# MLP output kernel: four factor sets in the result's places, two pools for the second half's factors, a later x

## The chip, the core and the metric

One core of a Trainium2 chip runs the whole layer. The time is the device time of one execution in microseconds (us), the median of the runs shown. A profile is one further execution, taken by the hardware profiler; its span runs from its first to its last instruction. PE is TensorE (matmuls), ACT is ScalarE, DVE is VectorE, POOL is GpSimd, and SP only issues transfers. The 16 DMA engines carry what the queues of SP and POOL issue.

## The reference

One decoder layer for 2048 positions of width 1024, all in float32:

```python
def squared_relu_mlp(h, w1, w2):
    a = jax.nn.relu(h @ w1)
    return (a * a) @ w2
...
        h = rms_norm(x, mix_norm_pre[l])
        m = hybrid_mixer(h, w_in[l], conv_w[l], conv_b[l], w_rgate[l], b_rgate[l],
                         w_igate[l], b_igate[l], lru_lambda[l], w_out[l])
        x = x + rms_norm(m, mix_norm_post[l])
        h = rms_norm(x, mlp_norm_pre[l])
        x = x + rms_norm(squared_relu_mlp(h, w_ff_in[l], w_ff_out[l]), mlp_norm_post[l])
```

The mixer joins dilated attention (8 heads) with a gated linear recurrence; its result goes through `w_out`, the out-projection. The MLP is 1024 to 4096 to 1024.

## The kernel before

**Halves.** After the mixer's input work, the layer goes through two halves of 1024 positions, hf = 0 and 1. `half(hf)` does the out-projection (`OutProj`, eight tiles t of 128 positions: the products L820 to L822, then two norms and the residual in `finish`) and the MLP's first product (`mlp_in`). `mlp_out` does the second product with `w2`. The second half's attention runs between, woven into the first half's `mlp_out`. So the order in time is: half 0, `mlp_out` 0 with the attention of half 1, out-projection of half 1, `mlp_in` 1, `mlp_out` 1.

**Matmuls.** Each float32 operand is split into a high part (a cast on ACT) and a low part (a subtraction on DVE or POOL, in place where the load landed), and a product is three matmuls: high by high, high by low, low by high. The 2 x 2 block products of the MLP are seven (m = 1 to 7) in the manner of Strassen. `mlp_in` works on pairs (0 to 15); of each it stores sums for the left factors, in DRAM: squares `sq` (L1061) and their sums `as` (L1062), both stored by POOL; the sums of `w2` (loaded L1071 as `w2s`) go to DRAM likewise.

**Sets.** `mlp_out` runs over 7 m x 16 j, a set each: a factor `a` and a factor `b`, 256 KB each, loaded by SP (L1128) into the place of the low part, then cast (L1218 in half 0, L54 in half 1) and subtracted (L1220, L55). Twelve matmuls use a set (L1135 to L1137). `load` picks the set's place by the number `at`: in half 0 one of four in turn, in half 1 one of sixteen by j. `sh.pair` and `sh.s` are places that also serve the factors of `mlp_in`, and `e` tiles are the half's own. A load can start once the last reader of its place is done:

```python
        at = j if hf else (m_at[m] * NJ + j) % 4
            if at < GB // 2:
                hi, lo = sh.pair(f"{x}{n}", (P, TB))
```

Loads run three sets ahead of the products, in both halves (`range(3)`, `made[i + 3]`). `take` moves a finished block from PSUM into the result rows `y`, whose eight tiles (128 x 1024) are allocated when half 0's product begins. `finish` squares them for the norm (L84), takes the root (L1171), scales (L1177), and lets POOL add the residual by a load (L1178) and store the result (L1179).

**What sets the order.** PE's order is as written. On ACT, DVE and SP the order is as written within `interleave` (the attention woven into `mlp_out` 0: eight sets first, FIRSTFILL = 32 products, then the units of the attention with their loads of masks, L365 and L367, of queries `qs`, L429, of keys `kh`, `kl`, L440, of values `vb`, L445, `va`, L461 and, on POOL, L466). Elsewhere a scheduler decides, by the readiness it reckons for each instruction; `issue_after` bars an instruction from an earlier position than another's. Each engine and each queue works in its order and waits where the next cannot start.

**Around the out-projection of half 1.** The output weights (`woL`, L756) are loaded among the last sets of `mlp_out` 0. `mix_columns` loads the mixer's result for a tile t (`m`, L794), ACT casts it (L54), POOL subtracts (L55). `OutProj` loads `x` (L828) and the gains (L811) and leaves their order to the scheduler.

Of the kernel before, what the change touches and what calls it, by code (L numbers as in the profile page):

```python
# [800 lines left out]
class OutProj:  # L801


    def __init__(self, tc, sh, p, scr, hf, wo, order, x, g2, g3):
        self.nc, self.sh, self.p, self.scr, self.hf, self.wo, self.order, self.x = tc.nc, sh, p, scr, hf, wo, order, x
        self.ahead = self.load(0)
        self.gb = []
        for n, src in (("2", g2), ("3", g3)):
            self.gb.append([sh.s(f"g{n}b{hf}_{i}", (P, TB)) for i in range(2)])
            for i, t in enumerate(self.gb[-1]):  # L810
                self.nc.sync.dma_start(out=t, in_=src[:, i * TB:(i + 1) * TB].partition_broadcast(P))  # L811
# [13 lines left out]
    def load(self, t):  # L825
        tt = self.hf * NQH + t
        xt = self.sh.w(f"xt{tt}")
        self.nc.sync.dma_start(out=xt, in_=self.x[tt * P:(tt + 1) * P, :])  # L828
        return xt
# [264 lines left out]

def mlp_out(tc, sh, p, cst, scr, hf, w2, g4, out):

# [12 lines left out]
    def factors(m, j):  # L1109
        parts = load(m, j)  # L1110
        for hi, lo in parts:
            split_there(nc, hi, lo)
        return [*parts[0], *parts[1]]

    def load(m, j):
        n = f"{hf}_{m}_{j}"
        at = j if hf else (m_at[m] * NJ + j) % 4
        parts = []
        for x, src in (("a", scr["a"][hf][j][:, SCR[m]]),
                       ("b", scr["w2"][j][:, plain[m]] if m in plain else scr["b"][j][:, SCR_B[m]])):  # L1120
            if at < GB // 2:
                hi, lo = sh.pair(f"{x}{n}", (P, TB))
            elif at < (GB + SB // 2) // 2:
                hi, lo = [sh.s(f"{x}{n}{y}", (P, TB), F32R) for y in "HL"]
            else:
                hi, lo = [p.tile([P, TB], F32R, tag="e", bufs=4 * NJ - 2 * GB - SB, name=f"{x}{n}{y}") for y in "HL"]
            with tc.issue_after(cst["load"].ins) if "load" in cst else contextlib.nullcontext():
                cst["load"] = nc.sync.dma_start(out=f32(lo), in_=src)  # L1128
            parts.append((hi, lo))
        return parts  # L1130
# [76 lines left out]
    if hf == 0:  # L1207
# [13 lines left out]

        for i in range(3):
            made[i] = load(*sets[i])
        for q in range(4 + LEAD):
            part(q)
        yield
        y += [p.tile([P, D], F32, tag=f"y{t}", name=f"y{hf}_{t}") for t in range(NQH)]
        for i, (m, j) in enumerate(sets):
            if j == 0:
                if m in (1, 2, 7):  # L1230
                    o = [sh.bank(x, f"o{hf}_{m}_{t}") for t, x in enumerate("AOAA")]
                if m == 2:
                    gains()
            if i + 3 < len(sets):
                made[i + 3] = load(*sets[i + 3])
            (ah, al), (bh, bl) = made[i]
            for t in range(n4):
                product(o[t], t, j, (ah, al, bh, bl), m in (1, 2, 7))
                part(4 * i + t + 4 + LEAD)
                if j == NJ - 1:  # L1240
                    take(m, t, o[t])
                    if m in (2, 4):
                        jobs.append(finish(t if m == 2 else n4 + t))
# [6 lines left out]
        return  # L1250
    ahead = [factors(order[0], j) for j in range(3)]
    yield
# [90 lines left out]
FIRSTFILL = 32  # L1343
LEAD = 4
NJ = FT // 2
KH = KT // 2
# [4 lines left out]
def trunk(tc, x, xT, g1, g2, g3, g4, w_in, conv_w, conv_b, w_r, b_r, w_i, b_i, lam, w_out, w1, w2,  # L1351
# [11 lines left out]
    with (  # L1363
# [112 lines left out]
        def half(hf, wo, mx):  # L1476

            with contextlib.ExitStack() as st:
# [3 lines left out]
                with contextlib.nullcontext():  # L1482

                    place = [po.tile([P, 4, TB], F32, name="place1")] if hf else [
                        po.tile([P, KT, P], F32, name=f"place0_{j}") for j in range(2)]
                    op = OutProj(tc, sh, po, scr, hf, wo, order, x, g2, g3)

# [38 lines left out]
        with per, tc.manual_schedule(engines={mybir.EngineType.PE}):  # L1526
# [13 lines left out]
            end = half(1, wo, ready)  # L1540
            with sb("y1", "left") as p:
                rest = mlp_out(tc, sh, p, cst, scr, 1, w2, g4, out)
                next(rest)
                run_all(end)
                run_all(rest)
# [63 lines left out]
```

## Time and profile before

| | us |
|---|---|
| median of the runs (3: 2290.64 to 2295.60) | 2292.86 |
| the profiled execution | 2294.62 |
| its span | 2292.5 |
| PE busy in the span | 2182.9 (95%) |
| DVE, ACT, POOL busy | 1507.5 (66%), 1233.6 (54%), 461.7 (20%) |

What remains of the profiled execution's time outside its span is 2.1 us. PE is busy for nearly the whole span, so a change shows in the time where PE waits or works at a lower granted clock; the chain of waits has PE on 62% of it and transfers on 11%. Busy time of PE counts a matmul for as long as it was in the array, so at half the clock the same work shows as more busy time.

### The profile page before, as it was taken

To read this page: it belongs to the slowest core of one execution; us is meant where nothing else is said; L and a number is where in the kernel's file an instruction comes from. 1 tells how busy PE (TensorE), PEld (TensorE's weight loads), DVE (VectorE), ACT (ScalarE), POOL (GpSimd) and SP (SyncE) were. 2 spreads that over 40 slices of the span, in tenths; PEclk is the share of its full clock that TensorE was granted. 3 is DMA by queue.
4 is the path that set the end of the run, shared out by engine and by line. 5 is a ranking of instruction groups with operands and counts; after the bars stand their busy time and mean duration, and the time that the engine had idled before them with its cause. 6 is when DMAs were issued, how large, how long until landed. Compare 5 with 4: busy or idle time off the path is not lost.

```text
span 2292.5 us, 30706 instructions
## 1 busy us (share of the span) xinstructions
PE 2182.9 (95%) x10264; PEld 1781.9 (78%) x10264; DVE 1507.5 (66%) x2900; ACT 1233.6 (54%) x2489; POOL 461.7 (20%) x549
## 2 busy tenths in 40 slices
PE   8999999989999899998999999989999999999998
PEld 6678888767788677786788787767878888788887
DVE  6757466897468876774667676766775656545556
ACT  7647465654344654553666666754455555554542
POOL 5543416454023100001001010123200000000003
PEclk9999999999999999998999999999999999999999
DMA  8365674637755667768677777777454444676665
GB/s 290 90 194 177 189 235 154 187 111 229 207 170 175 229 240 280 292 241 270 215 204 222 221 239 198 210 228 232 159 199 138 166 138 156 231 256 193 193 193 183
DMA packets 217550, 466.15 MB, mean 203 GB/s; under 512 B 22464, under 2 KB 77152, under 8 KB 211120
## 3 DMA queue, kind: packets, MB, share of 16 engines
q1 hardware_dynamic: 188624, 329.52, 46.2%
q0 software_dynamic: 28768, 134.66, 16.7%
q8 instruction: 81, 1.33, 0.2%
q14 instruction: 77, 0.63, 0.1%
HBM read 329.75 MB, written 151.13 MB: 210 GB/s over the span
## 4 chain that ended last, share of the span: by engine, by line
PE 62%; DMA 11%; DVE 9%; issue 7%; ACT 5%; POOL 2%; SPq 0%; DVEq 0%; POOLq 0%; ACTq 0%
PE o L1136 7%; PE o L1135 7%; PE o L1137 7%; PE za L996 3%; PE za L997 3%; PE za L998 3%; PE z L198 3%; PE z L199 3%; PE z L200 3%; PE m L822 2%; PE m L821 2%; PE m L820 2%; DMA w2s<-in_dram 2%; PE zc L996 2%; PE zc L997 2%
## 5 line engine op out<-in xcount | busy, mean ns | idle before, releaser
L198 PE MATMUL z<-hH,wH 128*128 128x512 f32 x640 | 261.0, 408 | 13.8 <-ACT wH L54 6.8
L199 PE MATMUL z<-hL,wH 128*128 128x512 f32 x640 | 259.4, 406 | 0.3 <-DVE hL L173 0.3
L200 PE MATMUL z<-hH,wL 128*128 128x512 f32 x640 | 258.4, 405 | 0.0
L198 PEld LDWEIGHTS z<-hH,wH 128*128 128x128 f32 x640 | 122.0, 191 | 49.0 <-ACT wH L54 7.1
L199 PEld LDWEIGHTS z<-hL,wH 128*128 128x128 f32 x640 | 121.9, 190 | 30.3 <-issue 4.1
L200 PEld LDWEIGHTS z<-hH,wL 128*128 128x128 f32 x640 | 121.9, 190 | 29.7 <-issue 4.6
L409 ACT ACTIVATE smB<-smB,stB 128x128 f32<-128x128 f32 (+3 forms) x128 | 71.6, 560 | 79.4 <-DVE stB L403 79.1
L1001 ACT ACTIVATE sq<-sq 128x512 f32<-128x512 f32 x93 | 58.8, 632 | 95.4 <-DVE sq L1005 95.2
L55 POOL TENSOR_TENSOR wL<-wraw,wH 128x512 fp32r<-128x512 f32 x58 | 82.5, 1438 | 77.8 <-ACT wH L54 75.0
L1061 POOL DMA_DIRECT2D sa<-sq x31 | 16.5, 532 | 401.8 <-ACT sq L1002 401.0
L55 DVE TENSOR_TENSOR tlB<-pT_B,thB 128x384 fp32r<-128x384 f32 x96 | 57.1, 599 | 49.6 <-ACT thB L54 45.5
L54 ACT CAST wH<-wraw 128x512 fp32r<-128x512 f32 (+1 forms) x81 | 46.9, 611 | 60.3 <-PE z L199 30.2
L409 ACT ACTIVATE sm<-sm,stA 128x256 f32<-128x256 f32 (+1 forms) x128 | 63.1, 495 | 29.3 <-DVE stA L403 29.0
L1002 ACT ACTIVATE sq<-sq 128x512 f32<-128x512 f32 x124 | 76.7, 629 | 2.4
L1072 DVE TENSOR_TENSOR w2s<-w2s 128x512 f32<-128x512 f32 x64 | 44.1, 689 | 34.2 <-DMA w2s<-in_dram 33.3
L1169 POOL TENSOR_TENSOR y<-y,g4b 128x512 f32<-128x512 f32 x8 | 13.0, 1654 | 262.8 <-ACT junk_y L84 262.8
L403 DVE CUSTOM_DVE_ANT_0 smB<-SB,mask_b 128x128 f32<-128x128 f32 (+3 forms) x128 | 59.4, 483 | 5.8 <-PE pT_B L377 5.4
L996 PE MATMUL za<-hHT,f_6H 128*128 128x512 f32 x128 | 51.7, 404 | 9.0 <-ACT sq L1035 8.9
L55 DVE TENSOR_TENSOR tlA<-pT,thA 128x512 fp32r<-128x512 f32 (+1 forms) x64 | 42.4, 670 | 26.3 <-ACT thA L54 26.0
L607 PE MATMUL oB<-thB,vb 128*128 128x256 f32 x192 | 48.6, 282 | 10.4 <-ACT thB L54 9.7
L54 ACT CAST thB<-pT_B 128x384 fp32r<-128x384 f32 x96 | 48.6, 510 | 18.3 <-PE pT_B L377 10.0
L377 PE MATMUL pT_B<-ident,smB 128*128 128x128 f32 x320 | 52.8, 282 | 2.7 <-DVE tlB L55 0.9
(567 smaller groups left out, 7082.3 us busy)
## 6 DMA issues: line engine op xcount, KB each, us to landing
sa<-as POOLq DMA_DIRECT2D x32, 1024.0 KB, 6.2
w1r<-in_dram SPq DMA_DIRECT2D x58, 512.0 KB, 4.5
sa<-sq POOLq DMA_DIRECT2D x31, 768.0 KB, 3.9
wraw<-in_dram SPq DMA_DIRECT2D x79, 256.0 KB, 3.6
w2s<-in_dram SPq DMA_DIRECT2D x16, 1024.0 KB, 8.1
sb<-w2s POOLq DMA_DIRECT2D x16, 1024.0 KB, 6.4
kh<-sk SPq DMA_DIRECT2D x24, 512.0 KB, 5.1
kl<-sk SPq DMA_DIRECT2D x24, 512.0 KB, 6.5
```

The lines of the kernel that those rows point to most:

```text
L54: return (nc.scalar.copy(out=hi, in_=src), (lo_eng or nc.vector).tensor_tensor(out=lo, in0=src, in1=f32(hi), op=ALU.subtract))
L55: (lo_eng or nc.vector).tensor_tensor(out=lo, in0=src, in1=f32(hi), op=ALU.subtract))
L198: pe.matmul(z, hi[:, k, :], hh, start=(k == 0), stop=False)
L199: pe.matmul(z, hi[:, k, :], hl, start=False, stop=False)
L200: pe.matmul(z, lo[:, k, :], hh, start=False, stop=(k == KT - 1))
L409: s.activation(out=sm[:, c0:c0 + w], in_=sm[:, c0:c0 + w], func=AF.Exp, scale=-1.0, bias=st[:, 0, u, cols[j]:cols[j] + 1], accum_out=st[:, ...
L996: pe.matmul(o, hi[:, k], bh[:, k], start=start and k == 0, stop=False, skip_group_check=True)
L997: pe.matmul(o, hi[:, k], bl[:, k], start=False, stop=False, skip_group_check=True)
L1002: s.activation(out=z, in_=z, func=AF.Square)
L1135: pe.matmul(o, ah[:, ts], bh, start=fresh and j == 0, stop=False, skip_group_check=True)
L1136: pe.matmul(o, ah[:, ts], bl, start=False, stop=False, skip_group_check=True)
L1137: pe.matmul(o, al[:, ts], bh, start=False, stop=j == NJ - 1, skip_group_check=True)
```

## The change

1. **First half.** The first four sets go into tiles with the tags of `y` (y0 to y7, the high part in the left half, the low part in the right). The result's own tiles are allocated when the first block is taken, after these sets have been read. Eight sets are loaded before the product begins, not three, and from the sixth set on the loads again run three ahead. The ring of four places turns by `(i + 3) % 4`.
2. **Second half.** The sets' places turn by `(j + 4) % 16`, the `e` tiles lie in two pools (`y1` and `z1`), and six sets are loaded ahead for the first product, not three.
3. **x of the second out-projection.** Its loads are barred from a position ahead of the last set's load of the first half.

```diff
@@ class OutProj @@
-    def __init__(self, tc, sh, p, scr, hf, wo, order, x, g2, g3):
+    def __init__(self, tc, sh, p, scr, hf, wo, order, x, g2, g3, late=None):
...
+        self.tc, self.late = tc, late
...
-        self.nc.sync.dma_start(out=xt, in_=self.x[tt * P:(tt + 1) * P, :])
+        with self.tc.issue_after(self.late.ins) if self.late else contextlib.nullcontext():
+            self.nc.sync.dma_start(out=xt, in_=self.x[tt * P:(tt + 1) * P, :])
@@ mlp_out, load @@
-        at = j if hf else (m_at[m] * NJ + j) % 4
+        i = m_at[m] * NJ + j
+        at = (j + 4) % NJ if hf else (i + 3) % 4
...
-            if at < GB // 2:
+            if not hf and i < 4:
+                t = p.tile([P, D], F32R, tag=f"y{2 * i + (x == 'b')}", name=f"{x}{n}")
+                hi, lo = t[:, :TB], t[:, TB:]
+            elif at < GB // 2:
...
-                hi, lo = [p.tile([P, TB], F32R, tag="e", bufs=4 * NJ - 2 * GB - SB, name=f"{x}{n}{y}") for y in "HL"]
+                q = pl if at < EARLY7 else p
+                hi, lo = [q.tile([P, TB], F32R, tag="e", bufs=4 * (EARLY7 - 4 if at < EARLY7 else NJ - EARLY7),
+                                 name=f"{x}{n}{y}") for y in "HL"]
@@ mlp_out, half 0 @@
-        for i in range(3):
+        for i in range(8):
             made[i] = load(*sets[i])
...
-        y += [p.tile([P, D], F32, tag=f"y{t}", name=f"y{hf}_{t}") for t in range(NQH)]
...
-            if i + 3 < len(sets):
+            if 5 <= i < len(sets) - 3:
                 made[i + 3] = load(*sets[i + 3])
...
+                    if not y:
+                        y += [p.tile([P, D], F32, tag=f"y{t}", name=f"y{hf}_{t}") for t in range(NQH)]
@@ mlp_out, half 1 @@
-    ahead = [factors(order[0], j) for j in range(3)]
+    ahead = [factors(order[0], j) for j in range(EARLY7 - 4)]
@@ calls @@
+EARLY7 = 10
-                    op = OutProj(tc, sh, po, scr, hf, wo, order, x, g2, g3)
+                    op = OutProj(tc, sh, po, scr, hf, wo, order, x, g2, g3, cst["load"] if hf else None)
-            with sb("y1", "left") as p:
-                rest = mlp_out(tc, sh, p, cst, scr, 1, w2, g4, out)
+            with sb("y1", "left") as pl, sb("z1", "left") as p:
+                rest = mlp_out(tc, sh, p, cst, scr, 1, w2, g4, out, pl)
```

Lines move by up to 11 in the changed file (L1128 is L1137 there, L1171 L1180, L828 L830).

**How it moves instructions.** PE's order stays. The names below are tiles with the product m and the set j (`a_1_6L`: factor a, m = 1, j = 6, low part); the half's number is left out.

SP, start of the first half's output product, before:

```order
L1128 DMA a_1_2L<-sa_2_123 128x512
L1128 DMA b_1_2L<-sw_171 128x512
L365 DMA mask_a_9591<-in_dram 128x256
L367 DMA mask_b_9593<-in_dram 128x512
L1128 DMA a_1_3L<-sa_3_124 128x512
L1128 DMA b_1_3L<-sw_172 128x512
L429 DMA qs_0_9633<-sq_0_75 128x1x1024
L1128 DMA a_1_4L<-sa_4_125 128x512
L1128 DMA b_1_4L<-sw_173 128x512
L440 DMA kh_0_9634<-sk_0_79 128x1x1024
```

The same place in the changed kernel, from the last factor of set 6 on (the other loads of sets 0 to 6 stand above, as one run behind the last load of `w2s`):

```order
L1137 DMA b_1_6L<-sw_175 128x512
L1137 DMA a_1_7L<-sa_7_128 128x512
L1137 DMA b_1_7L<-sw_176 128x512
L365 DMA mask_a_9613<-in_dram 128x256
L367 DMA mask_b_9615<-in_dram 128x512
L429 DMA qs_0_9641<-sq_0_75 128x1x1024
L440 DMA kh_0_9642<-sk_0_79 128x1x1024
L440 DMA kh_0_9642<-sk_0_83 128x1x1024
L440 DMA kl_0_9643<-sk_0_79 128x1x1024
L440 DMA kl_0_9643<-sk_0_83 128x1x1024
L1137 DMA a_1_8L<-sa_8_129 128x512
```

The loads of sets 3 to 7 stand ahead of the masks, and the loads of queries and keys come as one run behind set 7.

POOL there, before (`sb` is a store of `w2`'s sums):

```order
L1073 DMA sb_168<-w2s_9397 128x2048
L1061 DMA sa_14_135<-sq_14_9352 128x1536
L1062 DMA sa_14_135<-as_14_9572 128x2048
L466 DMA va_0_9779<-sv_0_91 32x4x256 x8
L1061 DMA sa_15_136<-sq_15_9404 128x1536
L1062 DMA sa_15_136<-as_15_9579 128x2048
```

and in the changed kernel:

```order
L1075 DMA sb_168<-w2s_9397 128x2048
L1063 DMA sa_14_135<-sq_14_9352 128x1536
L466 DMA va_0_9763<-sv_0_91 32x4x256 x8
L1064 DMA sa_14_135<-as_14_9594 128x2048
L1063 DMA sa_15_136<-sq_15_9404 128x1536
L1064 DMA sa_15_136<-as_15_9601 128x2048
```

The eight loads of `va` stand ahead of pair 14's store of `as`, where they stood behind it.

SP in the last product of the first half (m = 4), before; `swo` holds the output weights:

```order
L1128 DMA b_4_8L<-sb_161 128x512
L756 DMA woL_5_14251<-swo_206 128x1024
L828 DMA xt_14638<-in_dram 128x1024
L828 DMA xt_14700<-in_dram 128x1024
L1128 DMA a_4_9L<-sa_9_130 128x512
L1128 DMA b_4_9L<-sb_162 128x512
```

In the changed kernel, at the end of the same product; `g2b` and `g3b` are gains, `m_0` is the first tile of the second out-projection:

```order
L1137 DMA a_4_15L<-sa_15_136 128x512
L1137 DMA b_4_15L<-sb_168 128x512
L830 DMA xt_14630<-in_dram 128x1024
L830 DMA xt_14692<-in_dram 128x1024
L812 DMA g2b_0_14632<-in_dram 128x512
L812 DMA g2b_1_14633<-in_dram 128x512
L812 DMA g3b_0_14636<-in_dram 128x512
L812 DMA g3b_1_14637<-in_dram 128x512
L794 DMA m_0_0L<-smix_104 128x4x128
```

The two loads of x stand twenty loads of sets and weights later, and the four gains, which stood behind the loads of `m_2`, ahead of `m_0`.

ACT where the second out-projection begins, before; `junk_y` are the squares of the result's rows 4 to 7:

```order
L54 CAST m_0_0H<-m_0_0L 128x512
L54 CAST m_0_4H<-m_0_4L 128x512
L84 ACTIVATE junk_y_14540,ss_14536<-y_4_9599 128x1024
L54 CAST m_1_0H<-m_1_0L 128x512
L54 CAST m_1_4H<-m_1_4L 128x512
L1171 ACT_TABLE_LOAD
L1171 ACTIVATE ss_14537<-ss_14536,eps 128x1
L84 ACTIVATE junk_y_14562,ss_14558<-y_5_9600 128x1024
L1171 ACTIVATE ss_14559<-ss_14558,eps 128x1
L84 ACTIVATE junk_y_14576,ss_14572<-y_6_9601 128x1024
L1171 ACTIVATE ss_14573<-ss_14572,eps 128x1
L84 ACTIVATE junk_y_14590,ss_14586<-y_7_9602 128x1024
```

and in the changed kernel:

```order
L84 ACTIVATE junk_y_14532,ss_14528<-y_4_10133 128x1024
L1180 ACT_TABLE_LOAD
L1180 ACTIVATE ss_14529<-ss_14528,eps 128x1
L84 ACTIVATE junk_y_14554,ss_14550<-y_5_10134 128x1024
L1180 ACTIVATE ss_14551<-ss_14550,eps 128x1
L84 ACTIVATE junk_y_14568,ss_14564<-y_6_10135 128x1024
L1180 ACTIVATE ss_14565<-ss_14564,eps 128x1
L84 ACTIVATE junk_y_14582,ss_14578<-y_7_10136 128x1024
L54 CAST m_0_0H<-m_0_0L 128x512
L54 CAST m_0_4H<-m_0_4L 128x512
L1180 ACTIVATE ss_14579<-ss_14578,eps 128x1
L54 CAST m_1_0H<-m_1_0L 128x512
```

The casts of `m_0` stood ahead of all four squares and stand behind them now; those of `m_1` follow.

## Rows read from the trace of the kernel before

**Rows 1.** The table by stage (windows), core 0: from:to, us, busy time of each engine.
```profile
core 0: us, PE busy (x) PEld busy (x) DVE busy (x) ACT busy (x) POOL busy (x), PEclk, DMA share, GB/s
1020.00:1040.00 20.00, 20.00 (x88) 16.12 (x87) 11.28 (x19) 9.35 (x17) 1.59 (x3) 1.00 0.94 326
1040.00:1057.00 17.00, 17.00 (x77) 14.08 (x76) 10.00 (x16) 8.88 (x17) 0.53 (x1) 1.00 0.44 140
1057.00:1106.20 49.20, 35.74 (x133) 27.08 (x132) 19.53 (x37) 18.10 (x35) 6.58 (x12) 0.83 0.96 315
1520.00:1547.00 27.00, 19.83 (x77) 15.27 (x76) 15.68 (x21) 12.41 (x22) 14.26 (x18) 0.87 1.01 334
1974.40:1992.20 17.80, 13.86 (x52) 10.21 (x51) 7.45 (x12) 6.02 (x10) 1.18 (x3) 0.90 1.01 365
1992.20:2285.00 292.80, 292.80 (x1292) 242.17 (x1291) 168.06 (x279) 139.32 (x254) 19.31 (x12) 1.00 0.66 215
```

**Rows 2.** PE's timeline, first half's output product: start, us, line, operation, [idle before <-what ended it].
```profile
1072.46 0.80 PE L1135 MATMUL o<-b_3H,a_3H 128*128 128x512 f32 x1 [6.21 <-ACT b_3H L1218]
...
1081.58 0.51 PE L1135 MATMUL o<-b_4H,a_4H 128*128 128x512 f32 x1 [3.33 <-ACT b_4H L1218]
...
1094.64 0.28 PE L524 MATMUL S<-kh,qa 128*128 128x256 f32 x1
...
1101.84 0.82 PE L377 MATMUL pT<-ident,sm 128*128 128x128 f32 x3 [3.32 <-ACT sm L409]
```

**Rows 3.** PE's timeline from the first half's last product to the second out-projection.
```profile
1538.30 0.80 PE L1135 MATMUL o<-b_9H,a_9H 128*128 128x512 f32 x1 [6.28 <-ACT b_9H L1218]
...
1560.84 0.39 PE L820 MATMUL m<-woH,m_0H 128*128 128x512 f32 x1
...
1585.59 0.50 PE L822 MATMUL m<-woH,m_0L 128*128 128x512 f32 x1 [2.38 <-POOL m_0L L55]
...
1593.10 1.09 PE L918 MATMUL h2t<-ident,xt 128*128 128x128 f32 x8 [2.20 <-DVE xt L857]
```

**Rows 4.** PE's timeline, start of the second half's output product.
```profile
1983.53 0.80 PE L1135 MATMUL o<-b_2H,a_2H 128*128 128x512 f32 x1 [3.63 <-ACT b_2H L54]
```

**Rows 5.** SP's DMA queue around the start of the first half's output product.
```profile
1021.81 10.42 SPq L1071 DMA_DIRECT2D w2s<-in_dram  x2
...
1057.28 0.32 SPq L1128 DMA_DIRECT2D b_2L<-sw  x1
...
1062.94 1.71 SPq L1128 DMA_DIRECT2D b_4L<-sw  x1
...
1082.77 0.53 SPq L440 DMA_DIRECT2D kl<-sk  x1
```

**Rows 6.** POOL's timeline, the same place.
```profile
1058.14 0.53 POOL L1062 DMA_DIRECT2D sa<-as  x1 [0.27 <-DVE as L1059]
...
1062.58 0.55 POOL L466 DMA_DIRECT2D va<-sv  x1 [0.56 <-DMA sa<-sq]
1067.31 0.55 POOL L466 DMA_DIRECT2D va<-sv  x1 [4.18 <-DMA sa<-as]
```

**Rows 7.** SP's DMA queue, last product of the first half.
```profile
1522.39 0.81 SPq L828 DMA_DIRECT2D xt<-in_dram  x2
...
1524.10 0.67 SPq L1128 DMA_DIRECT2D b_9L<-sb  x1
```

**Rows 8.** ACT's timeline, last product of the first half.
```profile
1537.63 0.62 ACT L1218 CAST b_9H<-b_9L 128x512 fp32r<-128x512 f32 x1 [1.95 <-DMA b_9L<-sb]
```

**Rows 9.** ACT's timeline, start of the second out-projection.
```profile
1559.73 1.06 ACT L84 ACTIVATE junk_y<-y 128x1024 bf16<-128x1024 f32 x1 [2.61 <-DVE y L1145]
...
1561.93 1.28 ACT L1171 ACT_TABLE_LOAD   x1
...
1567.33 0.29 ACT L1171 ACTIVATE ss<-ss,eps 128x1 f32<-128x1 f32 x1
```

**Rows 10.** SP's DMA queue, start of the second half's output product.
```profile
1974.49 0.32 SPq L1128 DMA_DIRECT2D b_2L<-sw  x1
```

More of the change, by code (lines that the diff above doesn't have):

```diff
@@ L1092, with mlp_out @@
 TURNS = [(0, 0, 1, 1), (1, 1, 0, 0, 1, 1, 0, 1, 0, 0, 1, 1), (0, 0, 1, 1, 0, 0, 1, 1, 0, 1, 0, 0, 1, 1)]
-def mlp_out(tc, sh, p, cst, scr, hf, w2, g4, out):
+def mlp_out(tc, sh, p, cst, scr, hf, w2, g4, out, pl=None):
     nc = tc.nc
```

## The prediction

> **What bounds the kernel now.** I read the busy shares first: TensorE (PE) works 95% of the span, so the change can only save where PE stands still or runs at a low granted clock. A table by stage then shows where that is [rows 1]. From 1992.2 us on PE is full (292.80 of 292.80 us) at clock 1.00, 1292 matmuls in 292.80 us, 0.2266 us each; a set of 12 costs 2.72 us. It is also full up to 1057. Three stretches are not full, and in all three the DMA share is near 1: 1057 to 1106.2 (35.74 of 49.20 us, clock 0.83, DMA 0.96), 1520 to 1547 (19.83 of 27.00, clock 0.87, DMA 1.01) and 1974.4 to 1992.2 (13.86 of 17.80, clock 0.90, DMA 1.01). They are the start of the first half's output product, the place where loads of the output weights and of x meet its last sets, and the start of the second half's. PE's rows of these places give its idle time and what ended it [rows 2 to 4]: at four of the five larger pauses it is ACT's cast of a set's factor, which itself had waited for its load; the fifth is the softmax of the attention.
>
> So each stage is a transfer queue that PE runs dry on. Moving bytes to before the stage, where the DMA engines have time, helps; moving instructions in front of what PE waits for hurts. The change does both.
>
> **Start of the first half's output product.** Before, sets 0 to 2 are in place at 1057, and sets 3 to 7 (2.5 MB) are issued after the last of them, b_2L at 1057.28: b_4L left at 1062.94 and PE got to set 4 at 1081.58 [rows 2, 5]. PE idled 6.21 us before set 3, 3.33 before set 4 and 3.32 for the attention's softmax, 12.9 of the 13.46 us that the stretch lacks. After, all 16 loads of sets 0 to 7 stand behind the last w2 load (1021.81, 10.42 us for two [rows 5]) and ahead of the masks. Sets 0 to 3 wait only for products that PE has behind it by then, so they can go from 1032 on. Is there DMA time for them? The share is 0.94 up to 1040 and 0.44 from 1040 to 1057 [rows 1]: 0.56 x 17 = 9.5 us free. The 2.5 MB at 315 GB/s take 7.9. They fit.
>
> With eight sets there, PE needs nothing until 1057.0 + 8 x 2.72 = 1078.8. What is late next is the attention: its first product stood at 1094.64 [rows 2], behind two loads of kl, the second issued at 1082.77 [rows 5]. The second kl waits for the tile of pair 14's store "as". Before, that store was issued at 1058.14 and had landed at 1067.31, when the eighth va went; the seventh va had waited for the store "sq" in front of it and went at 1062.58 [rows 6]. After, "as" stands behind all eight va loads on POOL's queue, of which the last now waits for "sq": it is issued near 1064 and lands 9.2 us later, about 1073. Then kl and set 8 need some 8 us each in a busy queue (less than the 9.2 of "as", since they are smaller): 1082 to 1087. The attention's first product then comes some 8 to 12 us earlier than 1094.64. I take **8 us gained**. Bounds: 3 if kl's store slips another 5 us; above, the stretch's whole loss, 13.46 us idle plus what the clock cost. For the latter I take the last stretch: 13.86 - 52 x 0.2266 = 2.1 us for one pause, so 4 for two, in all 17.5.
>
> In the rows, b_4L's set came 18 us after its load left, while POOL's stores and va were in flight [rows 2, 5, 6]: transfers of the two queues slow each other. The Trainium skill, "DMA: Bandwidth & Descriptors", section "Queues, rings and completion order", says that a DMA engine takes turns between its queue rows, packet by packet. By that rule loads sent at 1032 take time from the stores of w2 and "as" that fill the queues until 1040, which delays the loads behind those stores, and the term would be near 0 instead of 8; the trace agrees with the sharing.
>
> I keep 8, because the free DMA time counted above is more than the loads need.
>
> **x of the out-projection.** Two loads of x, 512 KB each, stood at 1522.39, ahead of b_9L at 1524.10 [rows 7]. b_9L was cast only at 1537.63, and PE waited 6.28 us for it at 1538.30 [rows 3, 8]. After, both stand behind b_15L. 1 MB at 334 GB/s is 3.1 us of queue, plus some of the slow clock behind the pause. **Gain 3.5**; bounds 1 (POOL and the weights' loads hold the sets as before) and 6.5 (the pause goes).
>
> **The start of the second out-projection: a new wait.** Before, ACT casts m_0 first and then squares four rows of y (the first at 1559.73), with m_1's two casts (1560.79 to 1561.93) and a table load between; the fourth square is done when the fourth root starts at 1567.33 [rows 9]. PE passes from set 15 to L820 at 1560.84 without a gap [rows 3]. After, the casts of m_0 stand behind all four squares. Without m_1's casts (1.1 us) the fourth square ends at about 1566.2, and m_0's first cast 0.6 later, less some overlap: PE waits from 1560.84 to 1566.7, **5.9 us**. POOL's low half adds 0.4 (POOL now issues y's load between the subtracts). The clock falls after such a pause: 2.1 us by the last stretch, taken as 2.2. Lost 8.5. Given back: the 2.38 us for m_0L at 1585.59 and the 2.20 for x at 1593.10 [rows 3]; POOL's output stores no longer stand ahead of m_2, and x is scaled earlier beside a PE that comes later. **Net 3.9 lost**; bounds 0 (ACT gets to m_0 sooner, since it waits for less) and 9 (nothing is given back). The loads of m_0 also stand behind x and the four gain loads now, 2 MB, 6 us at 334 GB/s; they wait for set 13's place, 1560.84 - 2 x 2.72 = 1555.4, so they land by 1562 to 1565, still under the cover of the squares. If that cover went, they would be the next wait.
>
> **Start of the second half's output product.** Before, b_2L is issued at 1974.49 and later sets behind it [rows 10]; PE waited 3.63 us at 1983.53 [rows 4] and ran at clock 0.90. After, six sets go into places whose last readers stand 10 to 30 us ahead of the stage in PE's order, and six sets cover 6 x 2.72 = 16.3 us, nearly the whole stretch. 17.8 - 52 x 0.2266 = 6.0: **gain 6.0**; bounds 4 (a pause returns at set 6 or 7) and 7 (small waits at its edges go too). The loads for the stretch's end start 3 sets sooner, so I expect no dry spot behind it.
>
> **The rest.** PE's own order is unchanged; y's places for the first four sets cost no copy; the pools split one space. Nothing is added to any engine. I cost these at nothing.
>
> Sum: 8 + 3.5 - 3.9 + 6.0 = **13.6 us** less. The profiled execution took 2294.62, the median of the runs is 2292.86, 1.76 below; the sum puts the profiled one at 2281.0 and the median at **2279.3**.
>
> **Rivals.**
> A. The attention's loads eat the first term: the store "as" behind va lands 5 us later, the term is 3, the time 2284.3. For: the store needs two hand-overs on POOL. Against: va's are short.
> B. The first stretch becomes almost continuous: only the 3.32 us wait for the softmax stays, the term is 17.5 - 3.3 = 14.2 and the time 2273.1. For: DMA room before. Against: kl's store.
> C. Slower: the out-projection's new order lasts. If each of the seven later columns waits for its cast or subtract as m_2 did (2.38 us [rows 3]), the loss is 8.5 + 7 x 2.4 = 25.3 against gains of 17.5: 2300.7. It decides from a wait of 1.3 us for each, 9.0 in all. For: both POOL and SP are rearranged there. Against: later loads keep their distance.
> D. The early loads only take DMA time from the stores that fill the queues up to 1040 (share 0.94), and what stands behind those stores comes as much later: the first term is 0, the others stay, 5.6 less: 2287.3. For: the long landing of b_4L. Against: the share of 0.44 after 1040. This is what the rule of the Trainium skill's "DMA: Bandwidth & Descriptors", section "Queues, rings and completion order", would do here.
> E. The change doesn't do what it says: loads sit behind the w2 load on SP or behind their places until the old times, at both starts. Left are 3.5 - 3.9: 2293.3.
>
> **Chances.** Forecast 0.50, A 0.15, B 0.12, D 0.10, C 0.07, E 0.06. The smallest difference that measurements of this kernel can tell is 0.2%, 4.6 us. Faster by more: the forecast, A, B and most of D, 0.84. Within it: E and the rest of D, 0.09. Slower: C, 0.07. The range from 2267 to 2289 takes in A, B, D and the bounds of the terms, and leaves C and E out.
>
> **What would show it.** In the changed profile: no PE pause between 1057 and 1078 and the first attention product near 1083 to 1087; a pause near 2 us or less at set 9 of the last product; a pause of about 6 us before the first product of the second out-projection, ended by ACT's cast of m_0, with ACT's four squares just ahead; no pause and clock 1.00 in the first 18 us of the second output product. I am wrong if the masks or kl come later than before, if the pause at m_0 is missing or repeats at later columns, or if sets 4 to 7 still land after 1060.

## The result, and the profile after

The changed kernel takes 2280.45 us (median of 6 runs, 2269.94 to 2282.45) against 2292.15 for the one before (median of 6): the ratio is 0.9929, with an interval of 0.9910 to 0.9948. By the medians that is 11.7 us less. The ratio on record is not the quotient of these two medians (0.9949): it would make the gain 16.3 us, and its interval 11.9 to 20.6. 13.6 were forecast, and the range was 2267 to 2289. The profiled execution took 2279.51 us with a span of 2277.7, 14.8 less than before.

PE's timeline of the changed kernel, at the places of [rows 2 to 4] (start, us, line, operation, [idle before <-what ended it]):

```profile
1086.21 0.58 PE L524 MATMUL S<-kh,qa 128*128 128x256 f32 x1 [7.68 <-DVE qa L433]
...
1093.76 0.44 PE L377 MATMUL pT<-ident,sm 128*128 128x128 f32 x2 [1.89 <-ACT sm L409]
...
1531.18 0.79 PE L1144 MATMUL o<-b_10H,a_10H 128*128 128x512 f32 x1 [3.65 <-ACT b_10H L1227]
...
1557.38 0.80 PE L821 MATMUL m<-woH,m_0H 128*128 128x512 f32 x1 [5.81 <-ACT m_0H L54]
```

The two pauses before sets 3 and 4 (6.21 and 3.33 us) are gone; one pause of 7.68 us stands before the attention's first product, and the softmax costs 1.89 in place of 3.32. The pause before set 9 of the last product (6.28) is one of 3.65 before set 10. A new one of 5.81 stands before the second out-projection, and those at 1585.59 and 1593.10 (2.38 and 2.20) have no counterpart. At the start of the second half's output product nothing is left, where PE waited 3.63 us.

The table by stage says the same (columns as in [rows 1]); the rows are the stretch up to 1040, from there to the output product's start, the first 49.2 us of that product, 29.7 us from the first load of the output weights, and the first 18.5 us of the second half's output product:

```profile
1020.00:1040.00 20.00, 20.00 (x88) 16.17 (x87) 11.79 (x20) 9.49 (x17) 1.59 (x3) 1.00 0.97 338
1040.00:1056.50 16.50, 16.50 (x74) 13.47 (x73) 13.69 (x23) 14.46 (x28) 0.63 (x2) 1.00 0.74 271
1056.50:1105.70 49.20, 39.58 (x183) 32.50 (x183) 19.69 (x46) 17.05 (x38) 6.48 (x12) 0.93 0.93 298
1511.80:1541.50 29.70, 25.09 (x99) 19.65 (x98) 24.01 (x30) 16.80 (x31) 15.23 (x18) 0.89 1.01 328
1965.50:1984.00 18.50, 18.50 (x83) 15.30 (x83) 8.52 (x14) 7.27 (x12) 1.27 (x3) 1.00 1.02 379
```

Between 1040 and the product's start the DMA share rose from 0.44 to 0.74: the loads of sets 3 to 7 went there, as was reckoned, all but the last factor's (b_7L left at 1056.75). The first stage's PE time is 39.58 of 49.20 us instead of 35.74, its clock 0.93 instead of 0.83. The second half's start is full, at clock 1.00 instead of 0.90.

For the comparison of runs I divide the span by PE's own rows: from the output product's first matmul to the attention's first product and to set 15 of m = 1; then to the first load of the output weights (SP's row), to the first matmul of the out-projection, of `mlp_in` 1, of `mlp_out` 1, to its set 6, and to the end of the span.

| us | before | changed | first half only | second half only | x late only | `as` first | m_0 first | m_2 on DVE | va later | all | square order |
|---|---|---|---|---|---|---|---|---|---|---|---|
| start of the output product | 1057.1 | 1056.6 | 1054.6 | 1061.3 | 1054.0 | 1056.3 | 1052.1 | 1064.1 | 1058.9 | 1058.0 | 1065.5 |
| to the attention's first product | 37.56 | 29.65 | 29.73 | 37.02 | 37.80 | 30.01 | 29.44 | 29.75 | 23.68 | 23.53 | 23.48 |
| start to set 15 of m = 1 | 71.92 | 62.81 | 62.56 | 71.35 | 69.65 | 63.57 | 62.17 | 62.86 | 58.90 | 58.24 | 58.24 |
| to the first weight load | 390.08 | 392.49 | 392.44 | 390.77 | 392.02 | 393.10 | 389.95 | 390.96 | 392.37 | 390.40 | 389.03 |
| to the out-projection | 41.76 | 45.52 | 44.59 | 42.44 | 42.73 | 45.84 | 39.31 | 40.60 | 44.71 | 39.02 | 38.75 |
| of this, pause at its start | 0 | 5.81 | 3.08 | 0 | 3.08 | 5.82 | 0 | 0 | 5.81 | 0 | 0 |
| out-projection | 99.23 | 94.72 | 98.77 | 97.45 | 98.25 | 95.83 | 99.12 | 100.30 | 94.47 | 99.11 | 99.72 |
| `mlp_in` 1 | 314.22 | 313.46 | 313.32 | 315.41 | 313.94 | 313.95 | 314.14 | 313.86 | 313.90 | 315.29 | 315.31 |
| to set 6 of `mlp_out` 1 | 22.80 | 16.33 | 21.45 | 16.33 | 22.77 | 16.33 | 16.33 | 16.33 | 16.33 | 16.33 | 16.33 |
| from the product's start to the end | 1235.42 | 1221.14 | 1228.54 | 1229.34 | 1234.72 | 1224.41 | 1216.78 | 1220.54 | 1216.22 | 1214.36 | 1213.27 |

The third row contains the second. Ahead of the output product nothing differs between these kernels but the early loads of sets, and yet its start lies between 1052.1 and 1065.5, and between 1054.0 and 1061.3 in the three kernels without those loads. Whole times of single runs therefore differ by more than several of the edits are worth, and the verdicts on single edits below rest on the stages. The first stage took 69.7 to 71.9 us to set 15 in the three kernels that leave it alone, and the stage between set 15 and the weights, which no edit touches, 389.0 to 393.1; of its 2.4 us between before and changed I make nothing. Each column is one execution, and the other stages spread likewise: where the second half is left alone, set 6 of `mlp_out` 1 comes after 21.45 to 22.80 us.

### The profile page after: what moved, and what is told of

The parts are those of the page before. It is cut to its first block, busy times and chain, and to the rows that moved or that the text cites. A ratio compares the mean times of both kernels' runs of the same rounds, so it can differ in the third digit from the quotient of the medians.

```text
span 2277.7 us, 30713 instructions
## 1 busy us (share of the span) xinstructions
PE 2180.9 (96%) x10264; PEld 1782.2 (78%) x10264; DVE 1511.8 (66%) x2900; ACT 1232.6 (54%) x2489; POOL 461.2 (20%) x549
## 4 chain that ended last, share of the span: by engine, by line
PE 64%; DMA 10%; DVE 9%; issue 6%; ACT 5%; POOL 1%; SPq 1%; DVEq 0%; POOLq 0%; ACTq 0%
PE o L1145 8%; PE o L1144 8%; PE o L1146 8%; PE z L198 3%; PE z L199 3%; PE z L200 3%; PE za L999 3%; PE za L998 3%; PE za L1000 3%; DMA w2s<-in_dram 3%; PE m L823 2%; PE m L821 2%; PE m L822 2%; PE zc L998 2%; PE zc L999 2%
## 5 line engine op out<-in xcount | busy, mean ns | idle before, releaser
L821 PE MATMUL m<-woH,m_0H 128*128 128x512 f32 x128 | 51.7, 404 | 5.8 <-ACT m_0H L54 5.8
```

The source lines that it names most:

```text
L821: pe.matmul(o, mh, wh[:, ds], start=(k == order[0]), stop=False)
```

## The experiments

**One half of the change at a time.** The first half's part alone: the second half's places, its three sets ahead and x as before.

```diff
-    ahead = [factors(order[0], j) for j in range(EARLY7 - 4)]
+    ahead = [factors(order[0], j) for j in range(3)]
...
-        at = (j + 4) % NJ if hf else (i + 3) % 4
+        at = j if hf else (i + 3) % 4
...
-                    op = OutProj(tc, sh, po, scr, hf, wo, order, x, g2, g3, cst["load"] if hf else None)
+                    op = OutProj(tc, sh, po, scr, hf, wo, order, x, g2, g3)
...
```

> Only the first half's part of the change: four sets in the result's places, eight sets ahead; the second half's places and x as before. Theory: the first stage gains what the changed kernel gained there, 8 to 9 us; the pause of 6.28 us at set 9 of the last product stays at 4 to 6 us, since x is not late; the casts of m_0 stand behind two squares, so the pause there is 3 to 4 us, and the two later pauses (2.38 and 2.20 us) go or halve; the pause of 3.63 us in the second half stays. Time about 2284 (2282 to 2286). Rival (x's later place is what pushes the casts back): no pause at m_0, time 2280 or less.

Measured: 2286.68 us, ratio 0.9974 (0.9961 to 0.9988), 0.7 above the range given. To set 15 it gains 9.4 us, as the changed kernel does. The pause at set 9 of the last product stayed, at 5.55 us. The one before the out-projection is 3.08 us:

```profile
1554.15 0.50 PE L821 MATMUL m<-woH,m_0H 128*128 128x512 f32 x1 [3.08 <-ACT m_0H L54]
```

So the rival falls: the first half's part alone puts m_0's casts behind two squares. The second half's part alone:

```diff
-        for i in range(8):
+        for i in range(3):
             made[i] = load(*sets[i])
...
-        at = (j + 4) % NJ if hf else (i + 3) % 4
+        at = (j + 4) % NJ if hf else i % 4
...
-            if not hf and i < 4:
+            if False:
...
```

> Only the second half's part of the change: two pools, places turned by four, six sets ahead; the first half and x as before. Theory: the pause of 3.63 us at the start of the second half's output product and its slow clock go, and nothing else changes: 6 to 6.6 us faster than before, about 2286. Rival (the loads take the same DMA time, so the pause only moves to sets 6 to 10): 2 us or less faster, with a pause there.

Measured: 2286.43 us, ratio 0.9970 (0.9957 to 0.9983), 5.7 us less; 22.80 us to set 6 became 16.33, and all of `mlp_out` 1 behind it takes as long as before. The rival's pause did not come: with the DMA share at 1.02 the loads still keep ahead. Which of the turned places, the two pools and the six sets ahead does it was not taken apart. The same stretch in this kernel's table by stage:

```profile
1978.60:1995.00 16.40, 16.40 (x74) 13.56 (x73) 7.04 (x12) 5.94 (x10) 1.30 (x3) 1.00 1.02 378
```

And x alone, the kernel before with the third part of the change:

```diff
-        self.nc.sync.dma_start(out=xt, in_=self.x[tt * P:(tt + 1) * P, :])
+        with self.tc.issue_after(self.late.ins) if self.late else contextlib.nullcontext():
+            self.nc.sync.dma_start(out=xt, in_=self.x[tt * P:(tt + 1) * P, :])
...
```

> Only the third part of the change: x of the second out-projection behind the last set's load; all else as before. Two of the four squares stand ahead of m_0's casts in it. Theory: the last product gains 2 us (41.8 to 39.7 from the first weight load to its end), the pause before m_0 is 3 us, as with the first half's part alone, and the later pauses stay or shrink a little: the time is that of before within 1.5 us. Rival (the loads of x were what held the last product's sets): the pause of 6.28 us at set 9 shrinks to 2 or less, 4 us or more gained there, and the time falls by 2 to 3 us.

Measured: 2294.79 us against 2294.33 for the kernel before in the same series, ratio 1.0006 (0.9991 to 1.0021). From the first weight load to the end of the last product: 42.73 - 3.08 = 39.65 us instead of 41.76, a gain of 2.1, given back by the pause. The rival's 4 us did not come: the pause at set 9 went, but one of 3.40 us stands at set 10. As in the first half's part, two squares stand ahead of the casts here:

```profile
1556.68 1.04 ACT L84 ACTIVATE junk_y<-y 128x1024 bf16<-128x1024 f32 x1
...
1557.72 0.60 ACT L54 CAST m_0H<-m_0L 128x512 fp32r<-128x512 f32 x1
...
1558.38 0.80 PE L821 MATMUL m<-woH,m_0H 128*128 128x512 f32 x1 [3.08 <-ACT m_0H L54]
```

Each of the two parts moves the casts behind two of the four squares; together they move them behind all four. The pauses go with it: 3.08, 3.08 and 5.81 us.

**The order on POOL's queue.** The prediction's account of the first stage said that the store of `as` behind the `va` loads holds kl back, and kl the attention. The edit puts `va` behind it again:

```diff
-        g.dma_start(out=scr["a"][hf][j][:, 3:7], in_=A)
+        stored = g.dma_start(out=scr["a"][hf][j][:, 3:7], in_=A)
+        if j == NJ - 2:
+            sh.stored = stored
...
-                (g if hf else nc.sync).dma_start(out=f32(va[cs, hf + 4 * i:hf + 4 * i + 4, :]),
+                with tc.issue_after(cst["stored"].ins) if hf else contextlib.nullcontext():
+                    (g if hf else nc.sync).dma_start(out=f32(va[cs, hf + 4 * i:hf + 4 * i + 4, :]),
...
+                cst["stored"] = sh.stored
```

> The changed kernel, with POOL's eight va loads put behind pair 14's store of as again (the order of before there). Theory (the store's place on POOL's queue sets the attention's start): the store leaves about 1058 instead of 1063.3 and lands about 1068 to 1070 instead of 1075, kl leaves then, the attention's first product comes near 1079 to 1081 instead of 1086.2, and the pause of 7.68 us before it shrinks to 1 to 3. The time falls by 5 to 7 us, to about 2274. Rival (the DMA engines are full from 1057 on, and the order in which bytes go changes nothing): the first product stays at 1084 or later, the time within 2 us of the changed kernel's 2280.

Measured: 2280.42 us, ratio 0.9947 (0.9927 to 0.9966): nothing gained against the changed kernel. There POOL, SP's queue, ACT and DVE had these rows:

```profile
1063.26 0.56 POOL L1064 DMA_DIRECT2D sa<-as  x1 [1.23 <-DVE b_7L L1229]
...
1075.09 1.17 SPq L440 DMA_DIRECT2D kl<-sk  x2
...
1076.36 0.54 SPq L1137 DMA_DIRECT2D a_8L<-sa  x1
...
1083.84 0.62 ACT L1227 CAST a_8H<-a_8L 128x512 fp32r<-128x512 f32 x1 [21.61 <-DMA a_8L<-sa]
...
1085.13 0.69 DVE L1229 TENSOR_TENSOR b_8L<-b_8L,b_8H 128x512 fp32r<-128x512 f32 x1
1085.74 0.76 DVE L433 CAST qa<-qs 128x512 fp32r<-128x512 f32 x2
```

and with `as` first:

```profile
1057.94 0.53 POOL L1065 DMA_DIRECT2D sa<-as  x1 [1.55 <-DVE as L1062]
...
1066.88 1.16 SPq L440 DMA_DIRECT2D kl<-sk  x2
...
1069.91 0.33 SPq L1140 DMA_DIRECT2D a_8L<-sa  x1
...
1083.90 0.62 ACT L1230 CAST a_8H<-a_8L 128x512 fp32r<-128x512 f32 x1 [21.95 <-DMA a_8L<-sa]
...
1086.30 0.58 PE L525 MATMUL S<-kh,qa 128*128 128x256 f32 x1 [8.04 <-DVE qa L433]
```

The store left 5 us sooner, kl 8, set 8's load 6.5, and set 8 landed at the same time, so that its cast began at 1083.90 instead of 1083.84. DVE splits set 8 and then casts the queries, and PE's product comes behind that. Pair 15's two stores, which had left at 1064.07 and 1065.42, left at 1069.10 and 1069.65 instead. What is common to both runs is the sum: from the output product's start to the attention's first product the DMA engines moved, in the changed kernel and in this one (the rows below are two queues, q1 of SP and q0 of POOL, with packets, MB and share of the engines, and one transfer with the median us to landing),

```profile
DMA packets 3998, 9.71 MB, mean 328 GB/s; under 512 B 398, under 2 KB 1831, under 8 KB 3741
...
q1 hardware_dynamic: 3037, 4.97, 52.7%
q0 software_dynamic: 960, 4.72, 47.9%
...
kl<-sk SPq DMA_DIRECT2D x2, 512.0 KB, 7.4
```

```profile
DMA packets 3902, 9.66 MB, mean 322 GB/s; under 512 B 393, under 2 KB 1738, under 8 KB 3645
...
kl<-sk SPq DMA_DIRECT2D x2, 512.0 KB, 15.7
```

the same bytes at nearly the same rate, with a share of 1.01 and 1.02. With the engines full, this order did not matter; theory one falls, its rival stands.

**Fewer bytes before the attention.** If the sum decides, taking the eight `va` loads (1 MB) out of the stretch must shorten it. A copy of one column on POOL makes them wait for the queries; the four stores go ahead.

```diff
+        if hf and pr == 0:
+            with tc.issue_after(cst["stored"].ins):
+                for i in range(NBH):
+                    g.tensor_copy(out=va[:, hf + 4 * i, 0:1], in_=f32(qa[:, 0:1]))
         for c in range(NC):
...
-        g.dma_start(out=scr["a"][hf][j][:, 3:7], in_=A)
+        sh.stored = g.dma_start(out=scr["a"][hf][j][:, 3:7], in_=A)
...
```

> The changed kernel with the eight va loads (1 MB) taken out of the time before the attention's first product: pair 14's and 15's four stores go first on POOL's queue, then a copy of one column that waits for the queries qa, then va. Nothing is left out. The run with the as store ahead of va left the pause at 8.04 us although kl left 8 us earlier, so the order of bytes before the pause did not matter. Theory (the sum of the bytes in the queues before kl and set 8 sets the attention's start): 1 MB less at some 330 GB/s is 3 us, the first product comes 26 to 27 us after the output product's start instead of 29.65, the pause is 4 to 5 us, and the time falls by about 3 us, to 2277. Rival (kl and set 8 wait for something else, or the four stores now take va's place): 29 us or more, no gain; and if va then comes late, a pause before the first product with va.

The attention's first product comes at 23.68 us, 5.97 earlier, with a pause of 1.70 instead of 7.68; the softmax behind it takes 4.42 instead of 1.89, so at set 15 3.91 us are left (62.81 to 58.90).

```profile
1083.28 1.15 POOL L470 DMA_DIRECT2D va<-sv  x2 [0.27 <-POOL va L465]
...
1082.56 0.39 PE L528 MATMUL S<-kh,qa 128*128 128x256 f32 x1 [1.70 <-DVE qa L433]
...
1090.97 0.47 PE L377 MATMUL pT<-ident,sm 128*128 128x128 f32 x1 [4.42 <-ACT sm L409]
```

```profile
DMA packets 3624, 8.67 MB, mean 366 GB/s; under 512 B 269, under 2 KB 1712, under 8 KB 3367
...
q1 hardware_dynamic: 3047, 4.98, 57.5%
q0 software_dynamic: 576, 3.67, 41.7%
```

The median is 2276.88 us; its ratio, 0.9932 (0.9916 to 0.9949), cannot be told from the changed kernel's. The stage can: the attention's first product comes at 23.5 to 23.7 us in the three kernels with `va` later, and at 29.4 to 30.0 in the five that have the first half's part and `va` ahead. What is queued in front decides, but as time of the engines and not as bytes alone: `va` cost twice what its bytes say, 1.04 MB less, 5.9 us less, while the rate rose from 328 to 366 GB/s.

**The pause at m_0.** The loads of m_0 and m_1 are put ahead of x and the gains; the scheduler then casts m_0 first.

```diff
-                    op = OutProj(tc, sh, po, scr, hf, wo, order, x, g2, g3, cst["load"] if hf else None)
+                    op = OutProj(tc, sh, po, scr, hf, wo, order, x, g2, g3, sh.mixed if hf else None)
...
-                self.nc.sync.dma_start(out=t, in_=src[:, i * TB:(i + 1) * TB].partition_broadcast(P))
+                with tc.issue_after(late.ins) if late else contextlib.nullcontext():
+                    self.nc.sync.dma_start(out=t, in_=src[:, i * TB:(i + 1) * TB].partition_broadcast(P))
```

Here `sh.mixed` is the last load of `mix_columns`.

> The changed kernel, with the loads of m_0 and m_1 put ahead of x and the gains on SP's queue; the scheduler then puts the casts of m_0 ahead of the four squares on ACT again. Theory (ACT's order costs the pause): the pause of 5.81 us before the second out-projection goes, and with it 2.2 us of slow clock; of the 4.6 us that the later pauses of before took, up to half returns. The time falls by 5 to 8 us, to about 2274. Rival (the loads are late, not the casts): m_0 lands only when set 13's place is free and the queue has passed, a pause of 3 us or more stays, ended by the load, and the time falls by 3 us at most.

Measured: 2278.61 us, ratio 0.9928 (0.9908 to 0.9948). The 5 to 8 us did not come. The pause is gone (45.52 us became 39.31), but the out-projection takes 99.12 instead of 94.72: 6.2 us gained, 4.4 given back. A pause has come at the third tile, behind POOL's stores of the result:

```profile
1567.68 0.53 POOL L1190 DMA_DIRECT2D out_dram<-y  x1 [3.64 <-DMA y<-sx]
...
1568.23 1.28 POOL L55 TENSOR_TENSOR m_0L<-m_0L,m_0H 128x512 fp32r<-128x512 f32 x1
...
1569.56 0.79 PE L825 MATMUL m<-woH,m_0L 128*128 128x512 f32 x1 [3.64 <-POOL m_0L L55]
```

So m_2's low half was moved to DVE, in `mix_columns`, on top of this edit:

```diff
-        split_there(nc, hi, lo, nc.gpsimd)
+        split_there(nc, hi, lo, nc.vector if hf and t == 2 else nc.gpsimd)
```

> The run with m_0 and m_1 ahead of x, and m_2's low half subtracted on DVE instead of POOL, so that it does not stand behind POOL's stores of the result. In that run the pause of 5.81 us before m_0 went, but one of 3.64 us at m_2 took its place, and the out-projection took 99.1 us instead of 94.7. Theory (POOL's queue behind the stores is the second limit that the pause at m_0 had covered): the pause at m_2 goes, the out-projection takes 94 to 96 us without a pause at its start, and the time falls by 3 to 5 us against that run, to about 2275. Rival (the loads of m_2 or the norms behind them hold the stage): a pause of 2 us or more comes at m_2, m_3 or the first transpose, and the stage stays at 98 or more.

Measured: 2279.08 us, ratio 0.9944 (0.9927 to 0.9960); the out-projection took 100.30 us. The pause at m_2 is gone and one of 5.19 stands before the first transpose:

```profile
1591.04 1.33 PE L922 MATMUL h2t<-ident,xt 128*128 128x128 f32 x5 [5.19 <-DVE xt L861]
```

The rival is right. All edits together:

> Both edits of the two other runs of this call together with m_0 and m_1 ahead of x. If both theories hold: no pause at the out-projection's start, none at m_2, and 3 us less at the attention's start, about 2271 to 2273. If only the second holds, about 2275; if neither, 2278.

Measured: 2272.04 us (2267.54 to 2274.89), ratio 0.9907 (0.9890 to 0.9923). That is the time given for both theories, but by luck: the second falls, since the out-projection took 99.11 us. It is the lowest median of these kernels, though its interval still meets the changed kernel's: 6.8 us less than the changed one from the product's start on (1221.14 to 1214.36), of which 4.6 lie before set 15 and 2.1 between the first weight load and the end of the out-projection; 8.4 by the medians. Its pause before the first transpose was 3.90 us, and ACT had a square of x behind a square that waited for PE. One more edit changes that order:

```diff
-        last = s.activation(out=x2[:, half[1]], in_=m[1], func=AF.Square, accum_out=n1.second)
+        with self.tc.issue_after(self.xsq.ins) if self.late and t == 1 else contextlib.nullcontext():
+            last = s.activation(out=x2[:, half[1]], in_=m[1], func=AF.Square, accum_out=n1.second)
...
```

> The run with all edits, with one more: the second square of x for the first tile of the out-projection is put ahead of the second tile's square of the product on ACT's queue, as the changed kernel has it and the kernel before, and the runs with m_0 ahead of x, do not. In the run with all edits the pause before the first transpose was 3.90 us, ended by DVE's scaling of x, and ACT had that square queued behind a square that waited for PE and two casts that waited for a load. Theory (this place in ACT's queue is the third limit of the stage, and the changed kernel lost little at m_0 because its order there was better): the pause before the first transpose goes, the out-projection takes 94 to 96 us instead of 99.1, with no pause at its start; the time falls by 3 to 5 us, to about 2268. Rival (a fourth limit stands behind it, loads of m or DVE's norms): the stage stays at 98 or more, the time at 2271 or more.

Measured: 2273.01 us, ratio 0.9913 (0.9894 to 0.9932), not to be told from the run before; the stage took 99.72 us. This third explanation fell as well. ACT, DVE and PE in this run:

```profile
1567.40 0.62 ACT L54 CAST m_4H<-m_4L 128x512 fp32r<-128x512 f32 x1 [3.49 <-DMA m_4L<-smix]
...
1572.55 0.62 ACT L859 ACTIVATE xt<-x 128x512 f32<-128x512 f32 x1
...
1576.35 0.62 ACT L54 CAST m_0H<-m_0L 128x512 fp32r<-128x512 f32 x1 [2.16 <-DMA m_0L<-smix]
...
1579.53 0.62 ACT L54 CAST m_4H<-m_4L 128x512 fp32r<-128x512 f32 x1 [2.56 <-DMA m_4L<-smix]
...
1580.06 0.29 ACT L783 ACTIVATE nm_x<-nm_x 128x1 f32<-128x1 f32 x1
...
1581.76 0.75 DVE L866 SCALAR_TENSOR_TENSOR xt<-x,nm_x,g3b 128x512 f32<-128x512 f32 x1
...
1583.23 1.11 PE L927 MATMUL h2t<-ident,xt 128*128 128x128 f32 x4 [4.32 <-DVE xt L866]
```

The square is done at 1573, but the root that the norm needs (L783, 1580.06) stands behind the casts of the fourth tile, which wait 2.16 and 2.56 us for their loads, as the third tile's did for 3.49. The DMA share of these 36 us is 0.92:

```profile
1548.00:1584.00 36.00, 31.68 (x141) 26.06 (x140) 19.23 (x52) 16.03 (x36) 13.97 (x15) 0.97 0.92 274
```

The loads of m are then the next limit, behind x, the gains, and the result's rows that POOL adds and stores. That is read from the rows; no run took it away.

## Why the prediction was right, and where it was not

**First stage: 8 us forecast, 7.9 measured, for a reason that was half wrong.** The attention's first product came 29.65 us after the start instead of 37.56, at 1086.2 where 1083 to 1087 was given, and at set 15 9.1 us are gained. The loads of sets 3 to 7 found the DMA time that was counted (share 0.44 to 0.74), and no pause stands before 1078. One sign of being wrong did come, without harm: set 7 landed after 1060. Its last load left only at 1056.75, and ACT's cast waited for it until 1061.60, but PE needs that set at 1056.6 + 7 x 2.72 = 1075.6.

The step that failed is "The second kl waits for the tile of pair 14's store": it does wait, and kl left at 1075.09 where 1073 was reckoned, but the run with `as` first shows that this wait decided nothing. The transfers queued in front of set 8 and kl did. So it is partly luck that the time fell where it was given. The reading behind that step was off too: in the kernel before, PE came to the attention's first product without idle time [rows 2], so it stood there behind the products of sets 3 to 7 and not behind kl. Rival D's idea, that the queues share what there is, was right for this part of the stage and wrong for the loads it was put to. The Trainium skill, "DMA: Bandwidth & Descriptors", section "Queues, rings and completion order", says that a DMA engine takes turns between its queue rows. The trace agrees: with `as` first kl left 8.2 us sooner, beside POOL's transfers, and took 15.7 us to land instead of 7.4.

**x: 3.5 forecast, 2.0 measured.** 41.76 us became 45.52 - 5.81 = 39.71, and 39.65 with x alone. In all kernels, with the pause taken off, the stretch takes 41.5 to 42.4 us with x early and 38.8 to 40.6 with x late. The mechanism held (set 9's pause went, one at set 10 is left); the term was mis-sized, within its bounds of 1 and 6.5. I had added slow clock to 3.1 us of queue; but the stretch stays full without x: its DMA share is still 1.01, at 328 GB/s, and the clock 0.89, as in the same 29.7 us of the kernel before (from 1519.1).

**The start of the second out-projection: 5.9 us of pause forecast, 5.81 measured; net 3.9 forecast, 1.3 measured.** ACT's rows are those foreseen, the cast of m_0 behind the fourth square:

```profile
1555.69 1.04 ACT L84 ACTIVATE junk_y<-y 128x1024 bf16<-128x1024 f32 x1
...
1556.73 0.60 ACT L54 CAST m_0H<-m_0L 128x512 fp32r<-128x512 f32 x1
```

The failed step is the term "Lost 8.5. Given back: the 2.38 ... and the 2.20". Both came back, but the slow clock (2.2) and POOL's 0.4 did not add to the loss. The table by stage shows why, for the whole out-projection behind the pause, before and changed (columns as in [rows 1]):

```profile
1560.84:1660.07 99.23, 94.65 (x434) 78.05 (x432) 70.54 (x166) 42.93 (x114) 32.77 (x33) 0.98 0.59 181
```

```profile
1557.38:1652.10 94.72, 94.56 (x432) 78.04 (x433) 70.09 (x152) 38.02 (x104) 34.44 (x34) 0.98 0.60 176
```

PE is busy for 94.65 and 94.56 us, at the same mean clock of 0.98; only its idle time went, 4.58 us to 0.16. The kernel before had slow clock too, behind its two later pauses (0.90 from 1583.2 to 1600), and lost it with them; the changed kernel has it behind the pause at the start (0.90 from 1557.4 to 1575). The forecast gave back the pauses but not their slow clock. So the loss is 5.81 + 0.16 - 4.58 - 0.09 = 1.3.

That is one pair of executions. From the end of the last product, the pause at the start included, the out-projection takes 97.5 and 99.2 us in the two kernels that leave it as it was (before and second half only), and 100.3 to 101.7 in the three with the changed kernel's order (changed, `as` first, `va` later): a loss of 1 to 4 us. In all eleven kernels PE is busy 94.3 to 95.8 us of the stage and idle for 2.9 to 6.0, the pause at its start included: where one pause was taken away, another came (POOL's queue, ACT's order, the loads of m). The prediction did not say which part of the change moves the casts: each of two parts does, by two squares.

**Second half: 6.0 forecast, 6.5 measured.** All of 22.80 - 16.33; the small waits at the stretch's edges went too, which the upper bound had. Against the other two kernels that leave this part alone (21.45 and 22.77) it is 5.1 and 6.4.

Together: 9.1 to set 15, 2.0 for x, 6.5, less 1.3, is 16.3 by the stages; the parts that nothing touches took 2.0 back (2.4 in the attention, 0.4 at the end, 0.8 the other way in `mlp_in`), and from the product's start to the end 14.3 are left. Against the sum of 13.6, x was put too high by 1.5, the out-projection's loss too high by 2.6, the first stage, to set 15, too low by 1.1 and the second half by 0.5: 2.7 more than forecast, and 2.0 the other way in parts that nothing touches. That the sum comes within 1 us is luck in part: the terms were off by up to 2.6, in both directions, about as much as single executions of one stage differ. Rivals A, B, C and E did not occur: the attention's first product was neither as late as A has it nor without a pause, no pause repeats at later tiles, and all loads moved.

## What to carry to other kernels

Where a stage runs with its DMA engines full, count what is queued in front of the transfer that the next engine waits for, on all queues, before you argue about its order; here the order tried was worth nothing and 1 MB less was worth 6 us at the first product, 4 of them at set 15. A new pause at the start of a stage costs its length less the pauses behind it that it replaces, and its slow clock counts only if the stage had none before: compare PE's busy and idle time over the whole stage. When you take a pause away, expect the next one where it was covering it. When an edit moves loads, read the order of the engines that touch what was loaded: the scheduler put four squares ahead of a cast though no edit touched ACT.

## What the runs showed of the hardware

The eight `va` loads, 1.04 MB in runs of 1 KB (32x4x256 floats each), cost 5.9 us of a full DMA stretch (29.6 less 23.7), 176 GB/s, where the rest moved at 366 GB/s. By the shares of the two queues, the packets of POOL's queue took 4.3 us of the engines' time less (47.9% of 29.6 us, then 41.7% of 23.7), and those of SP's queue, with the same 4.97 MB, 2.0 less. So part of the cost was that the others went slower beside them. And a part of the program that is the same in three kernels, up to the first half's output product, took from 1054.0 to 1061.3 us in their profiled executions, with no change in it.
